# Two heads by turns: pairing the small TensorE products of a hybrid layer's state scan and attentions

## The chip, the cores and the metric

The kernel runs on one core of a Trainium2 chip. The metric is the device time of one execution in microseconds (us); lower is better. Five engines work side by side, each through its own stream of instructions and in its order: TensorE (PE; its weight loads are shown as PEld), VectorE (DVE), ScalarE (ACT), GpSimd (POOL) and SyncE (SP), which here issues most transfers.

## The reference, cut to what matters

Two layers of a diffusion backbone on 384 tokens (128 of context, 256 latent) of width 1024. In each layer one projection of the modulated tokens feeds three token mixers of 8 heads of 64 channels each, which are gated, merged and projected; a retrieval over 16384 experts (PEER) follows.

```python
# A: state scan, one chunk of 128 tokens, per head
y_diag = einsum('bhcls,bcshp->bclhp', cb * Lmat, xd)
y_off = einsum('bclhn,bchpn,bhcl->bclhp', Cc, states, exp(a_cs))
# B: neighbourhood attention, per head
s_loc = einsum('brcqhd,brcijhd->bhrcqij', qb, kb) * scale + bias
s_ctx = einsum('brcqhd,bshd->bhrcqs', qb, ctx_k) * scale
p = softmax(concatenate([s_loc, s_ctx]))
o = einsum(p[..., :n_loc], vb) + einsum(p[..., n_loc:], ctx_v)
# C: grouped attention, 8 query heads on 2 key heads
s = einsum('bqkgd,bskd->bkgqs', qi, k) * scale
o = einsum('bkgqs,bskd->bqkgd', softmax(s), v)
```

## The kernel before

Tokens lie in three tiles of 128 (t = 0 for the context, 1 and 2 latent); channels are folded in chunks of 128, so that a chunk holds two heads, one on partitions 0 to 63 and one on 64 to 127. `hybrid_step` runs `mixer` and `peer` for each of two layers. In `mixer` the projections go through `proj3` (L368 to L370): three products for each of 8 chunks, with the operands split into a high and a low part, each 128 by 128 of weights against 384 columns. `branch` (L675 and on) makes a gate with `proj3` and one mixer's output projection (L685 to L687) for eight chunks. All other products of the mixer are in plain 32-bit floats, and PE runs each of these as two passes: the profile counts two instructions for one call.

The state scan loops over t, then over two groups g, then over two chunks j of a group, then over the two heads h2 of a chunk. For each head DVE makes a weight tile `w1` in three operations (L617 to L619; tag `w1` has 2 buffers), and PE writes three products into the head's half of the PSUM tile `py`: the values against `w1` (L621; 128 rows, 64 columns of the array) and, for t > 0, the carried states of both directions (L626 and L627; 64 rows, 64 columns). DVE then reads both halves (L629).

The neighbourhood attention loops over chunks j, tiles t and heads h2: scores into a tile `ps` (L747, or L751 for the latent and L752 for the cached keys; 64 rows of the array, those of the head, by 128 columns), bias (L755) and copy (L757), `softmax_T` (L403 to L414: maximum, exponential, reciprocal, scaling, transposes on PE at L412, and the copy to `pT` on ACT at L414), and one to three products of the values with `pT` into the head's half of `po` (L761; 128 rows, 64 columns). The output tile `po` is opened ahead of both heads, and is copied out after both (L762).

The grouped attention does the same over c, t and h2, with heads 2c and 2c + 1. Both have the key head kv = c // 2, and so both take the same 64 rows of the array for their scores (L827, L831, L832); the value products are L836, the copy is L837.

`po`, `ps`, `py` and the score tiles of the scan (L589, L600) share the PSUM tag `pa` with 3 buffers; the transposes use `pt` with 2. The order on each engine is not written out: a planner sets it when the program is built. It goes by program order as priority, by what its own estimate of times says is ready, and by free buffers, and so it puts products of `proj3` and `branch`, and the modulation units (`adaln_unit`, L259 and L265), between the small ones. On the chip each engine follows that order and waits where an operand is late.

`blocked` lays the weights out before the launch; `w_branch` holds the output projections of the three mixers.

Of the kernel before, what the change touches and what calls it, by code (L numbers as in the profile page):

```python
# [18 lines left out]
D = 1024  # L19
KD = 8  # L20
NP, NS, NTOK = 128, 256, 384
DEPTH = 2
IN_COLS = 6672
HD = 64
# [131 lines left out]
def hybrid_step(ctx: ExitStack, tc: tile.TileContext, A, O):  # L156
    nc = tc.nc
    V, S, T, G = nc.vector, nc.scalar, nc.tensor, nc.gpsimd
# [259 lines left out]
    def mixer(l, stack, right, ps1):  # L418
# [4 lines left out]
        with ExitStack() as sc0:  # L423
            sp = pool(sc0, "ln")
# [159 lines left out]
        for t in range(3):  # L584
            cb = mk(sp, [128, 2, 128], "cb", bufs=2)
            for g in range(2):
                gs = slice(g * 64, g * 64 + 64)
                psc = mk(ps1, [128, 512], "pa")
                T.matmul(psc[:, :128], xc[gs, 4, t * 128:(t + 1) * 128], xc[gs, 5, t * 128:(t + 1) * 128], start=True, stop=True)  # L589
                S.copy(cb[:, g, :], psc[:, :128])  # L590
            ec = [mk(sp, [128, 4, 128], f"ec{d}") for d in range(2)] if t > 0 else None
            for g in range(2):
                gs = slice(g * 64, g * 64 + 64)
                E = []
                for d in range(2):
                    tri, msk = (triU, maskU) if d == 0 else (triL, maskL)
                    ps = mk(ps1, [128, 512], "pa")
                    for q in range(4):
                        h = d * 8 + g * 4 + q
                        T.matmul(ps[:, q * 128:(q + 1) * 128], a[:, t, h:h + 1].to_broadcast([128, 128]), tri, start=True, stop=True)  # L600
                    p4 = ps.rearrange("p (q l) -> p q l", q=4)
                    if t > 0:
                        S.activation(ec[d][gs], p4[gs], AF.Exp)
                        V.tensor_tensor(ec[d][gs], ec[d][gs], xc[gs, 5, t * 128:(t + 1) * 128][:, None, :].to_broadcast([64, 4, 128]), op=ALU.mult)
                    ex = mk(sp, [128, 4, 128], f"ex{d}")
                    V.tensor_tensor(ex, p4, msk[:, None, :].to_broadcast([128, 4, 128]), op=ALU.add)
                    for q in range(4):
                        h = d * 8 + g * 4 + q
                        S.activation(ex[:, q, :], ex[:, q, :], AF.Exp, bias=csn[:, t, h:h + 1])
                    E.append(ex)  # L610
                for j in (2 * g, 2 * g + 1):
                    py = mk(ps1, [128, 512], "pa")
                    for h2 in range(2):
                        h = 2 * j + h2
                        q = h % 4
                        w1 = mk(sp, [128, 128], "w1", bufs=2)
                        V.tensor_scalar(w1, E[0][:, q, :], dt[:, t, h:h + 1], None, op0=ALU.mult)  # L617
                        V.scalar_tensor_tensor(w1, E[1][:, q, :], dt[:, t, 8 + h:9 + h], w1, op0=ALU.mult, op1=ALU.add)
                        V.tensor_tensor(w1, w1, cb[:, g, :], op=ALU.mult)  # L619
                        o = py[h2 * 64:(h2 + 1) * 64, :128]  # L620
                        T.matmul(o, xnat[:, t, h * 64:(h + 1) * 64], w1, start=True, stop=(t == 0))  # L621
                        if t > 0:
                            jj = q // 2
                            sf = h0T if t == 1 else h1T
                            sb = h1T if t == 1 else h0T
                            T.matmul(o, sf[gs, 0, jj, h2 * 64:(h2 + 1) * 64], ec[0][gs, q, :], start=False, stop=False)  # L626
                            T.matmul(o, sb[gs, 1, jj, h2 * 64:(h2 + 1) * 64], ec[1][gs, q, :], start=False, stop=True)  # L627
                    y = xc[:, j, t * 128:(t + 1) * 128]
                    V.scalar_tensor_tensor(y, y, dvec[:, j:j + 1], py[:, :128], op0=ALU.mult, op1=ALU.add)  # L629
                    V.tensor_tensor(y, y, zT[:, j, t * 128:(t + 1) * 128], op=ALU.mult)  # L630
                    S.activation(sq[:, j, t * 128:(t + 1) * 128], y, AF.Square)
# [96 lines left out]
        for j in range(4):  # L728
            bias2 = []
            for h2 in range(2):  # L730
                h = 2 * j + h2
                bt = mk(sp, [128, 6, 64], "bt", bufs=3)
                for half in range(2):
                    dma(out=bt[half * 64:(half + 1) * 64], in_=AP(rpb, (h * 15 + 5 - half) * 31 - 48, [[1, 64], [31, 6], [1, 64]]))
                pb = mk(ps1, [128, 512], "pt")
                T.matmul(pb[:, :384], flip, bt.rearrange("p r c -> p (r c)"), start=True, stop=True)
                V.tensor_tensor(bt, pb[:, :384].rearrange("p (r c) -> p r c", r=6), colm[:, None, :].to_broadcast([128, 6, 64]), op=ALU.add)
                bias2.append(bt)
            for t in range(3):
                po = mk(ps1, [128, 512], "pa")  # L740
                for h2 in range(2):
                    h = 2 * j + h2
                    hs = slice(h2 * 64, h2 * 64 + 64)
                    ps = mk(ps1, [128, 512], "pa")
                    q = nq[hs, j, t * 128:(t + 1) * 128]
                    if t == 0:
                        T.matmul(ps[:, :128], q, nk[hs, j, 0:NP], start=True, stop=True)  # L747
                        pT = softmax_T(ps[:, :128], 128, sp, ps1)
                        vs = [nv[:, 0, :]]
                    else:  # L750
                        T.matmul(ps[:, 0:256], q, nk[hs, j, NP:NTOK], start=True, stop=True)  # L751
                        T.matmul(ps[:, 256:384], q, ckT[hs, j, :], start=True, stop=True)  # L752
                        sc = mk(sp, [128, 384], "nsc", bufs=2)
                        i0 = 2 - 2 * (t - 1)
                        V.tensor_tensor(sc[:, 0:256].rearrange("p (r c) -> p r c", r=4), ps[:, 0:256].rearrange("p (r c) -> p r c", r=4),  # L755
                                        bias2[h2][:, i0:i0 + 4, :], op=ALU.add)
                        S.copy(sc[:, 256:384], ps[:, 256:384])  # L757
                        pT = softmax_T(sc, 384, sp, ps1)
                        vs = [nv[:, 1, :], nv[:, 2, :], cv]
                    for i, vv in enumerate(vs):  # L760
                        T.matmul(po[hs, :128], vv[:, h * 64:(h + 1) * 64], pT[:, i, :], start=(i == 0), stop=(i == len(vs) - 1))  # L761
                V.tensor_copy(ysT[1][:, j, t * 128:(t + 1) * 128], po[:, :128])  # L762

        branch(0)
# [16 lines left out]
        for t in range(3):  # L781
# [31 lines left out]
            ps = mk(ps1, [128, 512], "pt")  # L813
            T.transpose(ps[:, :128], src[:, 8:10, :].rearrange("p h d -> p (h d)"), ident)
            V.tensor_copy(gkT[:, t * 128:(t + 1) * 128], ps[:, :128])
        for c in range(4):
            for t in range(3):
                po = mk(ps1, [128, 512], "pa")
                for h2 in range(2):
                    h = 2 * c + h2  # L820
                    kv, j = h // 4, h % 4
                    hs = slice(kv * 64, kv * 64 + 64)
                    ps = mk(ps1, [128, 512], "pa")
                    q = gqT[hs, j, t * 128:(t + 1) * 128]
                    if t == 0:
                        n = 128
                        T.matmul(ps[:, :128], q, gkT[hs, 0:NP], start=True, stop=True)  # L827
                        vs = [gn[:, 0, 640:768]]
                    else:
                        n = 384  # L830
                        T.matmul(ps[:, 0:256], q, gkT[hs, NP:NTOK], start=True, stop=True)  # L831
                        T.matmul(ps[:, 256:384], q, gcT[hs, :], start=True, stop=True)  # L832
                        vs = [gn[:, 1, 640:768], gn[:, 2, 640:768], gcv]
                    pT = softmax_T(ps[:, :n], n, sp, ps1)
                    for i, vv in enumerate(vs):
                        T.matmul(po[h2 * 64:(h2 + 1) * 64, :128], vv[:, kv * 64:(kv + 1) * 64], pT[:, i, :], start=(i == 0), stop=(i == len(vs) - 1))  # L836
                V.tensor_copy(ysT[2][:, c, t * 128:(t + 1) * 128], po[:, :128])  # L837
        branch(1)
        branch(2)
# [469 lines left out]
def blocked(inputs):  # L1309
# [14 lines left out]
    d["peer_wq"] = cut(d["peer_wq"], KD, 128)[:, :, 0]  # L1324
    d["w_mod"] = cut(d["w_mod"], 4, 256)
    d["w_out"] = cut(d["w_out"], 4, 256)
    d["w_branch"] = cut(d["w_branch"], 4, 256)[:, :, :, 0]
    return d

# [20 lines left out]
```

## Time and profile before

| | |
|---|---|
| time before, median of 3 runs | 3023.25 us (3023.19 to 3025.1) |
| the profiled execution | 3023.89 us, of which the span from first to last instruction 3021.8 us |
| busy in the span: PE, PEld, DVE, ACT, POOL | 2880.1, 2496.8, 2314.3, 1398.6, 820.5 us |
| mean granted TensorE clock | 0.982 of 2.4 GHz |
| layer 0: state scan, neighbourhood attention, grouped attention | some 112 to 185, 255 to 350, 355 to 442 us |
| layer 1: the same | some 1645 to 1702, 1755 to 1862, 1872 to 1958 us |

A row of the timeline gives the start and the time of merged neighbours, the engine, the line, what is written and read, the size of the weights (partitions by columns), the size of the moving operand, and how many instructions are merged. The time of one matmul goes from its start to its modelled end, and neighbours overlap, so the difference between two starts tells what one costs. In a view by line the columns are: count, busy us, mean ns, then idle time of the engine ahead of the group and who ended it.

### The profile page before, as it was taken

To read this page: it belongs to the slowest core of one execution; us is meant where nothing else is said; L and a number is where in the kernel's file an instruction comes from. 1 tells how busy PE (TensorE), PEld (TensorE's weight loads), DVE (VectorE), ACT (ScalarE), POOL (GpSimd) and SP (SyncE) were. 2 spreads that over 40 slices of the span, in tenths; PEclk is the share of its full clock that TensorE was granted. 3 is DMA by queue.
4 is the path that set the end of the run, shared out by engine and by line. 5 is a ranking of instruction groups with operands and counts; after the bars stand their busy time and mean duration, and the time that the engine had idled before them with its cause. 6 is when DMAs were issued, how large, how long until landed. Compare 5 with 4: busy or idle time off the path is not lost. (4 is left out here: it accounts for less than half of the span.)

```text
span 3021.8 us, 48665 instructions
## 1 busy us (share of the span) xinstructions
PE 2880.1 (95%) x17953; PEld 2496.8 (83%) x17953; DVE 2314.3 (77%) x4888; ACT 1398.6 (46%) x2861; POOL 820.5 (27%) x566
## 2 busy tenths in 40 slices
PE   7999999999889999999969999999987999999996
PEld 5888889878779999998858888898876899999985
DVE  3745554599669999998977456446996999999988
ACT  4544542324864444444445445432168444444443
POOL 0000000101334445554530000000023444455554
PEclk9999999999999999999979999999999999999998
DMA  7445322464999999999934332124469999999994
GB/s 245 156 152 153 84 65 90 154 227 146 334 343 418 393 388 396 396 390 369 385 100 153 119 96 76 64 91 133 154 212 366 412 395 392 396 394 392 395 365 166
DMA packets 299328, 767.09 MB, mean 254 GB/s; under 512 B 42770, under 2 KB 113874, under 8 KB 299090
## 3 DMA queue, kind: packets, MB, share of 16 engines
q1 hardware_dynamic: 225362, 495.51, 46.0%
q0 software_dynamic: 73728, 268.47, 23.4%
q8 instruction: 141, 2.31, 0.3%
q14 instruction: 97, 0.79, 0.1%
HBM read 726.92 MB, written 36.96 MB: 253 GB/s over the span
## 5 line engine op out<-in xcount | busy, mean ns | idle before, releaser
L1052 POOL DMA_INDIRECT prow<-in_peer_u,ei x256 | 361.5, 1412 | 765.2 <-DVE prow L1057 521.6
L1063 POOL DMA_INDIRECT prow<-in_peer_v,ei x256 | 379.8, 1483 | 352.4 <-DVE tn L1068 310.8
L222 ACT CAST vh<-w 128x1024 fp32r<-128x1024 f32 x256 | 268.8, 1050 | 367.2 <-issue 285.6
L1162 PE MATMUL hp<-hh,uh 128*128 128x256 f32 x1488 | 433.8, 292 | 0.0
L1163 PE MATMUL hp<-hl,uh 128*128 128x256 f32 x1488 | 417.2, 280 | 0.0
L1164 PE MATMUL hp<-hh,ul 128*128 128x256 f32 x1488 | 416.8, 280 | 0.0
L1240 PE MATMUL out<-vh,al 128*128 128x512 f32 x1024 | 400.4, 393 | 3.6 <-DVE al L1225 3.6
L1239 PE MATMUL out<-vl,ah 128*128 128x512 f32 x1024 | 398.4, 391 | 3.1 <-DVE vl L224 3.1
L1238 PE MATMUL out<-vh,ah 128*128 128x512 f32 x1024 | 391.0, 398 | 1.4 <-ACT ah L1223 1.4
L224 DVE TENSOR_TENSOR vl<-w,vh 128x1024 fp32r<-128x1024 f32 x256 | 315.5, 1232 | 62.0 <-ACT vh L222 61.3
L1068 DVE SCALAR_TENSOR_TENSOR tn<-prow,pact,tn 128x1024 f32<-128x1024 f32 x254 | 325.0, 1280 | 2.7
L1150 ACT CAST uh<-w 128x1024 fp32r<-128x1024 f32 x186 | 195.4, 1051 | 251.7 <-PE hp L1163 243.0
L368 PE MATMUL pp<-hh,uh 128*128 128x384 f32 (+1 forms) x848 | 300.1, 354 | 8.9 <-ACT uh L222 4.7
L1057 DVE SCALAR_TENSOR_TENSOR prow<-prow,tn 128x1024 f32<-128x1024 f32 x256 | 302.2, 1218 | 0.3 <-DMA prow<-in_peer_u,ei 0.3
L370 PE MATMUL pp<-hh,ul 128*128 128x384 f32 (+1 forms) x848 | 296.3, 349 | 1.4 <-POOL ul L224 1.4
L1159 PE MATMUL hp<-hs,w 128*128 128x256 f32 x1120 | 266.5, 394 | 30.7 <-DMA w<-in_peer_uT 30.7
L369 PE MATMUL pp<-hl,uh 128*128 128x384 f32 (+1 forms) x848 | 295.0, 348 | 0.2 <-DVE xr L494 0.2
L1162 PEld LDWEIGHTS hp<-hh,uh 128*128 128x128 f32 x1488 | 281.3, 189 | 0.0
L1163 PEld LDWEIGHTS hp<-hl,uh 128*128 128x128 f32 x1488 | 281.2, 189 | 0.0
L1164 PEld LDWEIGHTS hp<-hh,ul 128*128 128x128 f32 x1488 | 280.4, 188 | 0.0
L1159 PEld LDWEIGHTS hp<-hs,w 128*128 128x128 f32 x1120 | 216.1, 197 | 63.0 <-DMA w<-in_peer_uT 33.5
L351 POOL TENSOR_TENSOR res<-res,lg 128x384 f32<-128x384 f32 x6 | 9.6, 1594 | 939.7 <-ACT res L313 939.7
(405 smaller groups left out, 5843.0 us busy)
## 6 DMA issues: line engine op xcount, KB each, us to landing
w<-in_peer_uT SPq DMA_DIRECT2D x256, 512.0 KB, 6.9
w<-in_peer_v SPq DMA_DIRECT2D x256, 512.0 KB, 7.2
w<-in_w_in SPq DMA_DIRECT2D x104, 512.0 KB, 3.7
w<-in_w_mod SPq DMA_DIRECT2D x96, 512.0 KB, 4.4
gd<-w SPq DMA_DIRECT2D x64, 512.0 KB, 6.1
gt<-gd SPq DMA_DIRECT2D x64, 512.0 KB, 7.4
w<-in_peer_wq SPq DMA_DIRECT2D x32, 512.0 KB, 4.4
w<-in_w_branch SPq DMA_DIRECT2D x24, 512.0 KB, 3.7
```

The source lines that it names most:

```text
L224: e.tensor_tensor(lo, src, hi.bitcast(F32), op=ALU.subtract)
L1052: G.indirect_dma_start(out=row, out_offset=None, in_=utab, in_offset=bass.IndirectOffsetOnAxis(ap=ei[:, j:j + 1], axis=0))
L1057: V.scalar_tensor_tensor(row, row, 1.0, tn, op0=ALU.mult, op1=ALU.mult, accum_out=hd[:, j:j + 1])
L1063: G.indirect_dma_start(out=row, out_offset=None, in_=vtab, in_offset=bass.IndirectOffsetOnAxis(ap=ei[:, j:j + 1], axis=0))
L1068: V.scalar_tensor_tensor(acc, row, act[:, j:j + 1], acc, op0=ALU.mult, op1=ALU.add)
L1159: T.matmul(o, ut[0][:, k, :], hs[:, k, :], start=(k == 0), stop=(k == KD - 1))
L1162: T.matmul(o, uh[:, k, :], hh[:, k, :], start=(k == 0), stop=False)
L1163: T.matmul(o, uh[:, k, :], hl[:, k, :], start=False, stop=False)
L1164: T.matmul(o, ul[:, k, :], hh[:, k, :], start=False, stop=(k == KD - 1))
L1238: T.matmul(o, ah[:, ts], vh[:, ns], start=f, stop=False)
L1239: T.matmul(o, ah[:, ts], vl[:, ns], start=False, stop=False)
L1240: T.matmul(o, al[:, ts], vh[:, ns], start=False, stop=e)
```

## The change

The state scan makes both heads' weight tiles first (tag `w1` with 4 buffers) and then goes through three steps, each for both heads. Both attentions open two score tiles, compute the scores of both heads by turns, run the softmax of each, and only then open `po` and go through the value products by turns. In the grouped attention the pair is now one head of each key head (c and 4 + c), so that the two lie on other rows; its output chunk c holds those two heads, and `blocked` puts the rows of the third branch's weights into that order.

```diff
                 for j in (2 * g, 2 * g + 1):
                     py = mk(ps1, [128, 512], "pa")
-                    for h2 in range(2):
-                        h = 2 * j + h2
+                    w2 = []
+                    for h in (2 * j, 2 * j + 1):
                         q = h % 4
-                        w1 = mk(sp, [128, 128], "w1", bufs=2)
+                        w1 = mk(sp, [128, 128], "w1", bufs=4)
...
-                        o = py[h2 * 64:(h2 + 1) * 64, :128]
-                        T.matmul(o, xnat[:, t, h * 64:(h + 1) * 64], w1, start=True, stop=(t == 0))
-                        if t > 0:
-                            jj = q // 2
-                            sf = h0T if t == 1 else h1T
-                            sb = h1T if t == 1 else h0T
-                            T.matmul(o, sf[gs, 0, jj, h2 * 64:(h2 + 1) * 64], ec[0][gs, q, :], start=False, stop=False)
-                            T.matmul(o, sb[gs, 1, jj, h2 * 64:(h2 + 1) * 64], ec[1][gs, q, :], start=False, stop=True)
+                        w2.append(w1)
+                    sf, sb = (h0T, h1T) if t == 1 else (h1T, h0T)
+                    jj = (j % 2)
+                    for step in range(1 if t == 0 else 3):
+                        for h2, w1 in enumerate(w2):
+                            h = 2 * j + h2
+                            o, hc = py[h2 * 64:(h2 + 1) * 64, :128], slice(h2 * 64, (h2 + 1) * 64)
+                            if step == 0:
+                                T.matmul(o, xnat[:, t, h * 64:(h + 1) * 64], w1, start=True, stop=(t == 0))
+                            elif step == 1:
+                                T.matmul(o, sf[gs, 0, jj, hc], ec[0][gs, h % 4, :], start=False, stop=False)
+                            else:
+                                T.matmul(o, sb[gs, 1, jj, hc], ec[1][gs, h % 4, :], start=False, stop=True)
...
+            hv = [slice(h2 * 64, h2 * 64 + 64) for h2 in range(2)]
             for t in range(3):
-                po = mk(ps1, [128, 512], "pa")
-                for h2 in range(2):
...
+                pss = [mk(ps1, [128, 512], "pa") for _ in range(2)]
+                q = nq[:, j, t * 128:(t + 1) * 128]
+                keys = [(0, nk[:, j, 0:NP])] if t == 0 else [(0, nk[:, j, NP:NTOK]), (256, ckT[:, j, :])]
+                for o, kk in keys:
+                    for hs, ps in zip(hv, pss):
+                        T.matmul(ps[:, o:o + kk.shape[-1]], q[hs], kk[hs], start=True, stop=True)
+                pTs = []
+                for h2, ps in enumerate(pss):
...
+                po = mk(ps1, [128, 512], "pa")
+                for i, vv in enumerate(vs):
+                    for h2, hs in enumerate(hv):
+                        h = 2 * j + h2
+                        T.matmul(po[hs, :128], vv[:, h * 64:(h + 1) * 64], pTs[h2][:, i, :], start=(i == 0), stop=(i == len(vs) - 1))
...
+        hv = [slice(kv * 64, kv * 64 + 64) for kv in range(2)]
         for c in range(4):
             for t in range(3):
+                pss = [mk(ps1, [128, 512], "pa") for _ in range(2)]
+                q = gqT[:, c, t * 128:(t + 1) * 128]
...
+                for o, kk in keys:
+                    for hs, ps in zip(hv, pss):
+                        T.matmul(ps[:, o:o + kk.shape[-1]], q[hs], kk[hs], start=True, stop=True)
+                pTs = [softmax_T(ps[:, :n], n, sp, ps1) for ps in pss]
                 po = mk(ps1, [128, 512], "pa")
...
+                for i, vv in enumerate(vs):
+                    for hs, pT in zip(hv, pTs):
+                        T.matmul(po[hs, :128], vv[:, hs], pT[:, i, :], start=(i == 0), stop=(i == len(vs) - 1))
...
+    wb = d["w_branch"].copy()
+    wb[:, 2] = wb[:, 2].reshape(DEPTH, 2, 4, HD, D).transpose(0, 2, 1, 3, 4).reshape(DEPTH, 512, D)
+    d["w_branch"] = wb
     d["w_branch"] = cut(d["w_branch"], 4, 256)[:, :, :, 0]
```

## Rows read from the trace of the kernel before

**Rows 1.** Part 1 of the page: busy us, share of the span, instructions.

```profile
PE 2880.1 (95%) x17953; PEld 2496.8 (83%) x17953; DVE 2314.3 (77%) x4888; ACT 1398.6 (46%) x2861; POOL 820.5 (27%) x566
```

**Rows 2.** Windows of layer 0's state scan, neighbourhood and grouped attention.

```profile
core 0: us, PE busy (x) PEld busy (x) DVE busy (x) ACT busy (x) POOL busy (x), PEclk, DMA share, GB/s
112.00:185.00 73.00, 72.90 (x492) 58.35 (x490) 47.82 (x124) 37.79 (x102) 0.00 (x0) 1.00 0.35 118
255.00:350.00 95.00, 94.42 (x575) 76.41 (x574) 57.38 (x137) 42.63 (x108) 0.00 (x0) 1.00 0.41 108
355.00:442.00 87.00, 86.26 (x500) 71.15 (x500) 51.12 (x119) 40.84 (x96) 0.00 (x0) 1.00 0.19 61
```

**Rows 3.** Timeline of PE in the state scan, one pair of heads.

```profile
139.52 0.33 PE L369 MATMUL pp<-hl,uh 128*128 128x384 f32 x1
139.69 0.34 PE L370 MATMUL pp<-hh,ul 128*128 128x384 f32 x1
139.96 0.43 PE L621 MATMUL pa<-w,xnat 128*64 128x128 f32 x2
140.32 0.43 PE L626 MATMUL pa<-ec,h0T 64*64 64x128 f32 x2
...
140.90 0.43 PE L621 MATMUL pa<-w,xnat 128*64 128x128 f32 x2
...
141.84 0.44 PE L368 MATMUL pp<-hh,uh 128*128 128x384 f32 x1
142.12 0.34 PE L369 MATMUL pp<-hl,uh 128*128 128x384 f32 x1
```

**Rows 4.** Timeline of PE in the grouped attention.

```profile
391.50 0.43 PE L836 MATMUL pa<-pT,gn 128*64 128x128 f32 x2
391.86 0.45 PE L369 MATMUL pp<-hl,uh 128*128 128x384 f32 x1
...
392.41 0.65 PE L836 MATMUL pa<-pT,gn 128*64 128x128 f32 x4
392.90 0.38 PE L836 MATMUL pa<-pT,gcv 128*64 128x128 f32 x2
393.21 0.70 PE L831 MATMUL pa<-gkT,gqT 64*128 64x256 f32 x2
...
394.71 0.44 PE L368 MATMUL pp<-hh,uh 128*128 128x384 f32 x1
```

**Rows 5.** Timeline of PE in the neighbourhood attention: two visits with scores.

```profile
266.79 0.71 PE L751 MATMUL pa<-nk,nq 64*128 64x256 f32 x4
...
267.65 0.44 PE L369 MATMUL pp<-hl,uh 128*128 128x384 f32 x1
...
276.99 0.48 PE L751 MATMUL pa<-nk,nq 64*128 64x256 f32 x1
...
277.83 0.44 PE L369 MATMUL pp<-hl,uh 128*128 128x384 f32 x1
```

**Rows 6.** Timeline of PE at L589: two products together, and one alone.

```profile
131.23 0.49 PE L589 MATMUL pa<-xc 64*128 64x128 f32 x4
131.65 0.62 PE L259 MATMUL pp<-w,condT 128*32 128x256 f32 x2
...
157.39 0.49 PE L589 MATMUL pa<-xc 64*128 64x128 f32 x2
157.80 0.43 PE L621 MATMUL pa<-w,xnat 128*64 128x128 f32 x2
```

**Rows 7.** Timeline of PE at a modulation unit.

```profile
63.03 1.07 PE L259 MATMUL pp<-w,condT 128*32 128x256 f32 x16
64.03 0.44 PE L368 MATMUL pp<-hh,uh 128*128 128x384 f32 x1
```

**Rows 8.** Timeline of ACT: the probabilities of two heads in flight together.

```profile
272.16 0.48 ACT L414 COPY pT<-pt 128x384 f32<-128x384 f32 x1
...
275.60 0.48 ACT L414 COPY pT<-pt 128x384 f32<-128x384 f32 x1 [2.69 <-PE pt L412]
```

**Rows 9.** Groups by line: idle time ahead of L761's loads and of L617.

```profile
L761 PEld LDWEIGHTS pa<-pT,nv 128*64 128x64 f32 x160 | 16.2, 135 | 13.1 <-ACT pT L414 10.9 <-issue 1.8 <-ACT uh L222 0.3
...
L617 DVE TENSOR_SCALAR w<-ex,dt 128x128 f32<-128x128 f32 x48 | 12.5, 280 | 7.2 <-PE pa L621 7.2
```

More of the change, by code (lines that the diff above doesn't have):

```diff
@@ L738, in mixer @@
                 bias2.append(bt)
+            hv = [slice(h2 * 64, h2 * 64 + 64) for h2 in range(2)]
             for t in range(3):
-                po = mk(ps1, [128, 512], "pa")
-                for h2 in range(2):
[L742 to L745, printed above, removed]
+                pss = [mk(ps1, [128, 512], "pa") for _ in range(2)]
[6 more added lines that the diff above has]
+                for h2, ps in enumerate(pss):
                     if t == 0:
-                        T.matmul(ps[:, :128], q, nk[hs, j, 0:NP], start=True, stop=True)
-                        pT = softmax_T(ps[:, :128], 128, sp, ps1)
-                        vs = [nv[:, 0, :]]
-                    else:
-                        T.matmul(ps[:, 0:256], q, nk[hs, j, NP:NTOK], start=True, stop=True)
-                        T.matmul(ps[:, 256:384], q, ckT[hs, j, :], start=True, stop=True)
+                        pTs.append(softmax_T(ps[:, :128], 128, sp, ps1))
+                    else:
                         sc = mk(sp, [128, 384], "nsc", bufs=2)
@@ L757, in mixer @@
                         S.copy(sc[:, 256:384], ps[:, 256:384])
[L758 to L761, printed above, removed]
+                        pTs.append(softmax_T(sc, 384, sp, ps1))
+                vs = [nv[:, 0, :]] if t == 0 else [nv[:, 1, :], nv[:, 2, :], cv]
+                po = mk(ps1, [128, 512], "pa")
[3 more added lines that the diff above has]
+                        T.matmul(po[hs, :128], vv[:, h * 64:(h + 1) * 64], pTs[h2][:, i, :], start=(i == 0), stop=(i == len(vs) - 1))
                 V.tensor_copy(ysT[1][:, j, t * 128:(t + 1) * 128], po[:, :128])
@@ L815, in mixer @@
             V.tensor_copy(gkT[:, t * 128:(t + 1) * 128], ps[:, :128])
+        hv = [slice(kv * 64, kv * 64 + 64) for kv in range(2)]
         for c in range(4):
             for t in range(3):
-                po = mk(ps1, [128, 512], "pa")
[L819 to L836, printed above, removed]
+                pss = [mk(ps1, [128, 512], "pa") for _ in range(2)]
+                q = gqT[:, c, t * 128:(t + 1) * 128]
+                if t == 0:
+                    n, keys, vs = 128, [(0, gkT[:, 0:NP])], [gn[:, 0, 640:768]]
+                else:
+                    n, keys, vs = 384, [(0, gkT[:, NP:NTOK]), (256, gcT)], [gn[:, 1, 640:768], gn[:, 2, 640:768], gcv]
+                for o, kk in keys:
+                    for hs, ps in zip(hv, pss):
+                        T.matmul(ps[:, o:o + kk.shape[-1]], q[hs], kk[hs], start=True, stop=True)
+                pTs = [softmax_T(ps[:, :n], n, sp, ps1) for ps in pss]
+                po = mk(ps1, [128, 512], "pa")
+                for i, vv in enumerate(vs):
+                    for hs, pT in zip(hv, pTs):
+                        T.matmul(po[hs, :128], vv[:, hs], pT[:, i, :], start=(i == 0), stop=(i == len(vs) - 1))
                 V.tensor_copy(ysT[2][:, c, t * 128:(t + 1) * 128], po[:, :128])
```

## The prediction

> **What bounds the kernel now.** I read the page's busy times first. TensorE (PE) is busy for 95% of the span [rows 1], so the question is whether it is also what the changed stages wait for. The windows say yes: in the state products (SSD), the neighbourhood attention (NA) and the grouped attention (GQA) of layer 0, PE has work for 72.9 of 73, 94.4 of 95 and 86.3 of 87 us, at a granted clock of 1.00, which is the 2.4 GHz level, while VectorE (DVE) has 48, 57 and 51 us [rows 2]. The planner fills every gap between small products with the big 384-column products of the projections. So in these stages a microsecond taken out of PE's own stream comes off the time, as long as there is filling, and the filling is only moved, not used up. Layer 1 repeats the pattern.
>
> Busy time can't price the small products, since they overlap; I went to the timeline and took differences between starts. A filling product follows the last by 0.17 us (139.52 to 139.69). Then the state products of one pair of heads: 139.96 to 141.84, 1.88 us. One head takes 0.36 for its value product (L621, 128 rows by 64 columns of the array) and 0.58 for its two state products (L626 and L627, 64 by 64). Each change of shape costs: L621 starts 0.27 after the filling product before it and not 0.17, and the second filling product after the run starts 0.28 after the first. A visit of small products among the filling so costs about 0.20 on top of its own time [rows 3].
>
> The attention rows show the contrast on which the forecast stands. In GQA two heads that share a key head lie on the same 64 rows, and their scores run one after the other: L831 and L832 of one head, then of the next, 393.21 to 394.71, 1.50 us. In NA the scores of two neighbouring heads lie on opposite rows, and both, in the same shapes, are through in 0.86 us, 266.79 to 267.65 [rows 4, 5]. The same stands at L589: two products on opposite rows take 0.42 us and one alone takes 0.41 [rows 6]. For columns, 16 passes of 128 by 32 (L259), spread over four column groups, take 1.00 us, 0.06 each, where one pass alone has 256 columns to stream [rows 7]. A partner on other rows or columns is nearly free.
>
> **Part by part.**
>
> *GQA scores.* There are 4 head pairs, 2 late token tiles (t of 1 and 2) and 2 layers: 16 places. The new pairs have one head from each key head, so opposite rows: 1.50 becomes 0.86 as NA shows, 0.64 each, 10.2 us. The first tile's 128-column scores I leave at nothing.
>
> *NA scores.* These overlap today already, by luck of the order: head 1 of one tile runs with head 0 of the next. Three such visits per pair of heads cost 0.86, 0.84 (276.99 to 277.83) and about the same, 2.55; the new pairs cost 0.42 and twice 0.86, 2.14 [rows 5, 6]. That is 0.4 for 8 pairs, 3.3 us.
>
> *Value products of both attentions.* Today each head has its own run of three, 0.80 us (392.41 to 393.21), or one alone, 0.36 (391.50 to 391.86) [rows 4]. Afterwards the two heads come by turns into the two column halves of one PSUM tile. But the probabilities of the two heads aren't ready together: their copies (L414) start at 272.16 and 275.60, 3.44 us apart [rows 8]. The planner issues what is ready, so I expect the first head's first product alone (0.36), filling, and then the other five side by side in the time of three (0.80): 1.16 against 1.60 today. That saves 0.44 for 16 places in each attention, 14.1 us. The lower end is nothing (the heads stay apart), the upper is 0.80 and one visit less, 1.00 each, with 0.56 for each of 16 first tiles, 41 us. I take 14, since the 3.44 us row is the nearest one.
>
> *State products.* There are 16 pairs with carried state (4 pairs, 2 tiles, 2 layers). The two value products now stand side by side, then the forward and the backward state products of both heads. If both weight tiles are ready, a pair costs 0.36 + 0.58 = 0.94, and 0.94 is saved; if the first value product goes alone, 0.36 + 0.94 and a second visit, and 0.38 is saved. Today the two heads' runs stand without filling between them, and DVE waits 7.2 us for L621 to give a weight buffer back [rows 3, 9], which the change from 2 to 4 buffers takes away; both speak for the first, and DVE's turn per head for the second. I take the middle, 0.66, so 10.5 us (6 to 15). No row has two 64 by 64 products on the same rows and different columns. If they don't overlap, 0.44 of each 0.58 comes back, 7 us; the nearest row, L259, says they do. The first tile's value products I leave at nothing.
>
> *What costs nothing.* The third branch's weight rows are put in order before the launch; the chip loads the same bytes. The output tile is opened later, at its first product. Scores of the next tile need the two freed score tiles out of three, and today they already come right behind a value run [rows 4, 5]; the filling covers a late one, 0.17 a piece. If that cover went, each wait would count in full.
>
> *Sum.* 10.2 + 3.3 + 14.1 + 10.5 = 38 us. The profiled execution took 3023.9 us (span 3021.8), 0.6 over the median. 3023.9 - 38 is 2986.
>
> **Rivals.**
>
> *The planner keeps the heads apart* (the change doesn't do what it says). If products into different halves of a tile may pass each other, the planner takes the first head's remaining products when they are ready and the turns never happen. For it: the 3.44 us. Against it: it must then treat two writes into one PSUM tile as independent, which no row shows. Only the scores gain, 13.5 us, with little more: 3009.
>
> *All pairs meet.* If PE lags behind the planner's clock, both heads are ready when it comes. For it: state runs without filling between them [rows 3]. Against: 3.44 us. Then value products save 41, states 15, scores 13.5: 70 us, 2954.
>
> *Passes in strict order.* A product here is two passes. If the passes of one product stand together in PE's stream and PE starts them in that order only, a pair can share one pass and not both, and each block of pairs takes one pass more, 0.12 us (four passes of L836 take 0.49, 392.41 to 392.90). For some 128 blocks (48 of scores, 48 of values, 32 of states) that is 15 us: 3001. Against it: the second product of L589 costs 0.01 and not 0.12 [rows 4, 6]. The rows don't show the order of the passes in the stream. The Trainium skill, "TensorE: Matmul & The Clock Gate", Part 3, states this rule: matmuls start and end strictly in program order, and overlap only where a later one sits on another tile of the array. The rows of L589 speak against it as far as they go.
>
> *PE stands at the second head* (slower). PE issues in order. If the planner thinks the second head's probabilities earlier than the chip has them, PE waits in front of the second product of the turn, with the next scores and all filling queued behind it. The price is the wait itself: 48 places (24 per layer). It decides from 38 / 48 = 0.8 us each; at a third of the 3.44 us, 1.15 us, it costs 55 and gives 3041. Against it: before L761's 160 weight loads with the new values only 10.9 us are waits for these copies today [rows 9], since the planner puts filling there.
>
> **How the numbers follow.** Forecast (2986, with 2970 to 3000 its own range) 0.48; heads kept apart 0.20; all meet 0.12; strict order 0.05; no change beyond 0.2%, about what a measurement can tell (6 us: the gain is given back by a reshuffled order elsewhere) 0.08; PE stands 0.07. The first four are faster, 0.85. The range reaches from the case where all meet to the one where the heads stay apart, 2950 to 3012, and leaves out some 0.18.
>
> **What would show it.** Right: L831 and L832 of two heads in about 0.86 us; value products in one run of ten passes of about 0.80 behind one of two; state runs of a pair at 0.94 to 1.30; PE still 99% busy in the three stages, each shorter: over both layers SSD by about 10, NA by 10, GQA by 17 us. Wrong: value runs of six passes as today (planner); runs of twelve (all meet); idle time of PE in front of L761's or L836's successors that names the copy L414 (PE stands); a GQA score pair still at 1.5 us would say that opposite rows don't overlap there and would take the base from the forecast.

## The result, and the profile after

The changed kernel takes 3002.74 us (median of 4 executions, 2999.95 to 3004.09) against 3023.22 beside it, a ratio of 0.9933 (95% interval 0.9915 to 0.995). The forecast was 2986 in a range of 2950 to 3012: the direction is right, and about half of the 38 us came. The profiled execution took 3004.09 us (span 3002.3), 19.8 less than that of before.

Part 1 of the page, and windows of the three stages of layer 0, with two stretches inside the scan (columns as in [rows 2]). The last row is from the profile of before, the ten microseconds behind the scan window of [rows 2]:

```profile
PE 2855.6 (95%) x17953; PEld 2479.3 (83%) x17953; DVE 2309.1 (77%) x4888; ACT 1396.8 (47%) x2861; POOL 824.8 (27%) x566
```

```profile
112.00:181.00 69.00, 66.86 (x445) 54.83 (x444) 44.42 (x125) 36.09 (x98) 0.00 (x0) 0.89 0.29 95
137.60:147.80 10.20, 10.16 (x47) 8.04 (x48) 3.98 (x13) 2.18 (x8) 0.00 (x0) 0.52 0.26 99
175.60:182.40 6.80, 6.80 (x29) 6.47 (x26) 2.04 (x4) 3.17 (x5) 0.00 (x0) 0.50 0.22 72
255.00:345.00 90.00, 88.47 (x563) 70.02 (x562) 55.20 (x133) 42.70 (x110) 0.00 (x0) 1.00 0.36 101
355.00:435.00 80.00, 79.92 (x507) 66.18 (x506) 48.57 (x115) 38.63 (x91) 0.00 (x0) 1.00 0.21 67
```

```profile
185.00:195.00 10.00, 10.00 (x60) 8.34 (x60) 1.97 (x5) 3.28 (x5) 0.00 (x0) 0.83 0.17 54
```

Against [rows 1, 2]: PE lost 24.5 us of busy time with the same 17953 instructions. The grouped attention is still full (79.92 of 80 us); in the neighbourhood attention 1.5 us are idle. In the scan PE idles for some 2 us, and two stretches of 10.2 and 6.8 us run at a granted clock of 0.50 to 0.52, the 1.2 GHz level. The first has no counterpart before, where the scan's window showed 1.00. The second has a shorter one: behind the scan of before the clock is 0.83 over 10 us, which makes some 3.4 us at half.

The timeline of PE in the grouped attention, at the place that answers to [rows 4] (L836 are now the scores, L841 the value products):

```profile
369.73 0.43 PE L841 MATMUL pa<-pT,gn 128*64 128x128 f32 x2
370.10 0.70 PE L836 MATMUL pa<-gkT,gqT 64*128 64x256 f32 x2
370.72 0.54 PE L841 MATMUL pa<-pT,gn 128*64 128x128 f32 x5
...
371.11 0.48 PE L841 MATMUL pa<-pT,gcv 128*64 128x128 f32 x3
371.52 0.48 PE L836 MATMUL pa<-gkT,gqT 64*128 64x256 f32 x1
371.53 0.48 PE L836 MATMUL pa<-gcT,gqT 64*128 64x128 f32 x2
...
372.37 0.44 PE L368 MATMUL pp<-hh,uh 128*128 128x384 f32 x1
```

The value products came as forecast: the first head's first product alone (369.73, two passes), then ten passes of both heads (370.72 to 371.52, 0.80 us). But between the two stands one score product of the *next* tile (370.10), the first keys of one head, alone for 0.62 us. Its partner comes only behind the block, beside the first head's second keys (371.52 to 372.37). The pair of scores is torn. Over both attentions and layers, 22 of the 32 pairs with 384 keys are torn like this, and 4 of the 16 with 128 keys. From 369.73 to 372.37 the place takes 2.64 us. The forecast's own pieces for it are 0.36 + 0.80 + 0.86 = 2.02.

The timeline of PE in the scan: one pair at full clock, as [rows 3] showed it at 1.88 us, and, earlier, the first pair with carried state:

```profile
137.64 0.54 PE L628 MATMUL pa<-w,xnat 128*64 128x128 f32 x4 [2.06 <-DVE w L619]
138.11 0.69 PE L630 MATMUL pa<-ec,h0T 64*64 64x128 f32 x4
...
139.64 0.52 PE L369 MATMUL pp<-hl,uh 128*128 128x384 f32 x1
139.96 0.52 PE L370 MATMUL pp<-hh,ul 128*128 128x384 f32 x1
...
170.56 0.44 PE L628 MATMUL pa<-w,xnat 128*64 128x128 f32 x4
170.93 0.43 PE L630 MATMUL pa<-ec,h1T 64*64 64x128 f32 x4
171.20 0.39 PE L632 MATMUL pa<-ec,h0T 64*64 64x128 f32 x4
171.51 0.44 PE L369 MATMUL pp<-hl,uh 128*128 128x384 f32 x1
```

Timeline of DVE ahead of the wait, and a row of PE's waits (engine, line, what for; us in total, times, longest):

```profile
135.16 1.21 DVE L224 TENSOR_TENSOR ul<-w,uh 128x1024 fp32r<-128x1024 f32 x1
...
137.21 0.48 DVE L619 TENSOR_TENSOR w<-w,cb 128x128 f32<-128x128 f32 x2
```

```profile
PE pt L741 <- DMA bt<-in_na_rpb: 2.9, 4, 0.9
```

At 170.56 the whole pair takes 0.95 us, half of before. At 137.64 PE had stood still for 2.06 us for a weight tile (L619), ahead of the pair's first product: DVE first does a weight split (L224) and then makes both heads' tiles step by step (L619 x2), so that the first is hardly earlier than the second. Right behind the wait the clock falls: filling products follow each other in 0.32 us (139.64 to 139.96), not 0.17. The last row is in the neighbourhood attention, where PE waits for the transfer of a bias table; before there was no such wait.

To see where the time went, I took the differences between the starts of neighbouring matmuls, put each to the line of the earlier one, and summed over both layers (differences over 3 us count as 3; a wait goes to the row of the product ahead of it). The last two columns are experiments below, named by what they change.

| us between starts | before | after | late head first | late head first, in the scan too |
|---|---|---|---|---|
| value products | 62.4 | 50.4 | 37.0 | 37.3 |
| scores | 51.0 | 49.3 | 34.1 | 34.2 |
| state scan, the three lines | 35.1 | 26.7 | 26.3 | 20.6 |
| filling (`proj3`, `branch`) | 609.7 | 599.9 | 601.9 | 605.1 |
| L600, bias (L741), transposes (L412) | 51.4 | 60.2 | 57.9 | 56.3 |
| modulation units | 104.2 | 104.4 | 105.6 | 103.1 |

Value products gave 12.0 (forecast 14.1), the scan 8.4 (10.5), the scores 1.7 (13.5): 3.6 less in the grouped attention and 1.8 more in the neighbourhood attention. The row of the value products holds the 2.9 us of waits for the bias tables, so the products alone gave some 15. The filling gave 9.8 that no term had, as it is broken by small products at 227 places and no longer at 288.

### The profile page after: what moved, and what is told of

Read it like the earlier page. It is cut to its first block, busy times and chain, and to the rows that moved or that the text cites. A ratio compares the mean times of both kernels' runs of the same rounds, so it can differ in the third digit from the quotient of the medians.

```text
span 3002.3 us, 48719 instructions
## 1 busy us (share of the span) xinstructions
PE 2855.6 (95%) x17953; PEld 2479.3 (83%) x17953; DVE 2309.1 (77%) x4888; ACT 1396.8 (47%) x2861; POOL 824.8 (27%) x566
## 4 chain that ended last, share of the span: by engine, by line
PE 74%; DVE 11%; DMA 6%; ACT 4%; issue 4%; POOL 1%; SPq 0%; POOLq 0%; ACTq 0%; DVEq 0%
PE hp L1167 6%; PE out L1243 6%; PE hp L1169 6%; PE out L1245 6%; PE hp L1168 6%; PE out L1244 6%; PE pp L368 5%; PE pp L369 5%; PE pp L370 5%; PE hp L1164 4%; DMA w<-in_peer_uT 3%; PE pp L947 2%; ACT ol L1004 2%; DVE vl L224 2%; DVE tn L1073 2%
## 5 line engine op out<-in xcount | busy, mean ns | idle before, releaser
L224 DVE TENSOR_TENSOR vl<-w,vh 128x1024 fp32r<-128x1024 f32 x256 | 315.8, 1234 | 62.7 <-ACT vh L222 44.0
L224 DVE TENSOR_TENSOR ul<-w,uh 128x1024 fp32r<-128x1024 f32 x124 | 149.8, 1208 | 162.2 <-ACT uh L222 158.2
```

The source lines that it names most:

```text
L224: e.tensor_tensor(lo, src, hi.bitcast(F32), op=ALU.subtract)
```

## The experiments

The theory: the order that the planner wrote keeps the products themselves as cheap as forecast and loses the scores, since an early first value product leaves a hole that a next score product falls into. Rivals: the products don't pair as the rows of before say; a lack of PSUM tiles tears the scores; the scan takes the gain back.

**Halves of the change.** First the attentions as changed with the scan of before, then the reverse.

```diff
# attentions only: the state products go back to one head after the other
-                    for step in range(1 if t == 0 else 3):
-                        for h2, w1 in enumerate(w2):
+                    for h2 in range(2):
...
# scan only: both attentions and the weight rows as before
-                for o, kk in keys:
-                    for hs, ps in zip(hv, pss):
+                for h2 in range(2):
...
```

Attentions only, expected:

> Both attentions as in the changed kernel, the state scan as before. Theory A (the gain is TensorE time taken out of the attentions; the scan's 8 us of product time are eaten by its stall of 2 us per layer and by the half-rate clock behind it): 3000 to 3005 us, as fast as the whole change. Rival B (the gain is the scan's, and the attentions' value gain is given back by the split scores): 3010 to 3018 us.

Scan only, expected:

> The state scan as in the changed kernel, both attentions as before. Theory A: 3018 to 3026 us, no gain, with the stall of about 2 us before L628 and longer stretches at half clock in the trace. Rival B: 3008 to 3015 us.

Measured: 3003.83 us (0.9933, interval 0.992 to 0.9947) and 3019.22 us (0.9986, 0.9976 to 0.9997), beside 3023.72. The attentions alone bring what the whole change does. The scan alone brings 4.5 us, though its products start 9.1 us closer (26.0 against 35.1), and on top of the attentions it shows nothing (3002.74 against 3003.83). Its trace has the same wait at L628, 4.1 us in two places, with half clock behind it. That these take back the rest fits; no run here separates them.

**The late head first.** The turns of the value products begin with the second head, whose probabilities come last. So nothing can start before both are there.

```diff
-                    for h2, hs in enumerate(hv):
+                    for h2, hs in reversed(list(enumerate(hv))):
...
-                    for hs, pT in zip(hv, pTs):
+                    for hs, pT in reversed(list(zip(hv, pTs))):
```

> The changed kernel with one edit: in the value turns of both attentions head 1 comes ahead of head 0, so that no value product is ready before both heads' probabilities are, and the next tile's scores follow a whole block. Theory (the split of the turn is what held the gain down): a place with t > 0 costs 2.64 us now (369.73 to 372.37) and then 0.80 + 0.86; 0.98 less at 32 places, so 31 us under the changed kernel, 2967 to 2975 us. Rival (the longer way from one tile's scores to the next's bounds the stage): TensorE idle before the value products, time within 5 us of the changed kernel, 2998 to 3008 us. Rival (turns as such pay, adjacency doesn't): no forecast from it here.

Measured: 2973.0 us (0.9834, 0.9818 to 0.9851). The timeline of PE at a place of the grouped attention in this kernel:

```profile
377.59 0.66 PE L841 MATMUL pa<-pT,gn 128*64 128x128 f32 x8
378.08 0.39 PE L841 MATMUL pa<-pT,gcv 128*64 128x128 f32 x4
378.40 0.70 PE L836 MATMUL pa<-gkT,gqT 64*128 64x256 f32 x4
378.93 0.39 PE L836 MATMUL pa<-gcT,gqT 64*128 64x128 f32 x4
379.25 0.44 PE L691 MATMUL pb<-ya,uh 128*128 128x384 f32 x1
```

All twelve value passes take 0.81 us, all eight score passes 0.85, together 1.66 against 2.64. The same products in one other order are worth 29.7 us (3002.74 to 2973.0). The table puts 13.4 of it to the values and 15.2 to the scores. No pair of scores is torn in this trace, and the 26 torn ones account for the 15.2: 22 times the 0.62 us of a lone first product (370.10 to 370.72) and 4 times 0.41 with 128 keys (377.50 to 377.91, below). So it was not the products that failed to pair.

**The late head first in the scan too.** As above, and in addition:

```diff
-                        for h2, w1 in enumerate(w2):
+                        for h2, w1 in reversed(list(enumerate(w2))):
```

> As the run above, and in the scan's first step too head 1 comes ahead of head 0, so that no pair of value products is split (half of the 16 pairs with state are now). Theory: 0.4 to 0.6 us for 8 pairs, 3 to 5 us under the run above, and more if the stall of 2 us per layer and the half-clock stretch behind it go: 2957 to 2970 us. Rival (VectorE makes the weights too late, so a pair that waits for both only stalls more): equal to the run above or up to 8 us over it.

Measured: 2969.96 us (0.9824, 0.981 to 0.9838), the fastest version of this study, though its executions (2967.46 to 2974.61) overlap those of the one above. Its scan gives 14.5 us between starts against before (20.6). Its waits of PE (engine, line, what for; us in total, times, longest) and the row of the timeline at the same place:

```profile
PE pp L368 <- ACT nq L655: 4.6, 2, 2.3
...
PE pa L628 <- DVE w L619: 0.6, 2, 0.3
```

```profile
135.87 0.45 PE L368 MATMUL pp<-hh,uh 128*128 128x384 f32 x1 [2.28 <-ACT nq L655]
```

The wait for the weight tile went from 4.1 us (2 times) to 0.6, and another took its place ahead of a filling product, 2.28 us once in each layer. Stretches at half clock remain (6.8 us from 137.6 on). The medians differ by 3.0 us, of the some 6 that the products gained; with the overlap of the executions the 3.0 are not clear of the scatter.

**Is it the number of PSUM tiles?** The changed kernel with 4 buffers for the scores and outputs (tag `pa`) and 1 for the transposes:

```diff
-{"pp": 2, "pt": 2, "pa": 3, "pb": 1}
+{"pp": 2, "pt": 1, "pa": 4, "pb": 1}
```

> The changed kernel with 4 buffers of the PSUM tag pa and 1 of pt (3 and 2 before). Asked of the trace alone: if the next tile's scores are torn apart because a score tile is missing, both heads' scores now stand whole behind the first value product, about 0.86 us; if they are torn apart because the rest of the value turn outranks them, a lone score product still stands between the first value product and the other five. The time I expect within 10 us of the changed kernel either way, since one transposing buffer less delays the softmaxes.

Measured: 3002.78 us, one execution. The timeline of PE in its grouped attention, ahead of a tile with 384 keys and ahead of one with 128:

```profile
364.91 0.70 PE L836 MATMUL pa<-gkT,gqT 64*128 64x256 f32 x2
365.54 0.54 PE L841 MATMUL pa<-pT,gn 128*64 128x128 f32 x5
...
366.34 0.48 PE L836 MATMUL pa<-gkT,gqT 64*128 64x256 f32 x1
...
372.39 0.43 PE L841 MATMUL pa<-pT,gn 128*64 128x128 f32 x2
372.75 0.49 PE L836 MATMUL pa<-gkT,gqT 64*128 64x128 f32 x4
373.18 0.54 PE L841 MATMUL pa<-pT,gn 128*64 128x128 f32 x5
```

In the changed kernel the place with 128 keys looked like this:

```profile
377.50 0.48 PE L836 MATMUL pa<-gkT,gqT 64*128 64x128 f32 x2
377.91 0.54 PE L841 MATMUL pa<-pT,gn 128*64 128x128 f32 x5
...
378.71 0.48 PE L836 MATMUL pa<-gkT,gqT 64*128 64x128 f32 x2
```

So the rival holds for the short scores: with a buffer more, both heads' 128-key scores stand whole in the hole (372.75), at 16 of 16 places instead of 12. It doesn't hold for the long ones: one head's first product still stands alone (364.91), at 26 of 32 places, and was so at 22. The scores of this trace add up to 52.4 us, not fewer than the 49.3 of the changed kernel. A buffer more doesn't mend the tearing as a whole; what does is that the block can't begin early.

**Is it the turns, or only the block?** Late head first, but three products of one head and then three of the other:

```diff
-                for i, vv in enumerate(vs):
-                    for h2, hs in reversed(list(enumerate(hv))):
+                for h2, hs in reversed(list(enumerate(hv))):
+                    for i, vv in enumerate(vs):
```

> As late_first, but the value products are written head by head: all three of head 1, then all three of head 0, next to each other. Theory (adjacency in one shape of the array is what pays; TensorE starts products on other columns side by side even when they stand three calls apart): a value block still takes about 0.80 us, 2969 to 2978 us. Rival (passes start strictly in the order of the stream): the block takes about 1.3 to 1.4 us, 0.55 more at 32 places, 17 us over late_first, 2987 to 2994 us.

Measured: 2979.75 us (0.9856, 0.9837 to 0.9875), between both theories. The timeline of PE:

```profile
378.02 0.71 PE L841 MATMUL pa<-pT,gn 128*64 128x128 f32 x6
378.50 0.27 PE L841 MATMUL pa<-pT,gcv 128*64 128x128 f32 x1
378.56 0.27 PE L841 MATMUL pa<-pT,gn 128*64 128x128 f32 x1
378.61 0.27 PE L841 MATMUL pa<-pT,gcv 128*64 128x128 f32 x1
378.67 0.27 PE L841 MATMUL pa<-pT,gn 128*64 128x128 f32 x1
378.78 0.38 PE L841 MATMUL pa<-pT,gcv 128*64 128x128 f32 x2
379.09 0.70 PE L836 MATMUL pa<-gkT,gqT 64*128 64x256 f32 x4
```

The block takes 1.07 us, where turns take 0.81 and two heads apart 1.60 (0.80 each, [rows 4]). For 32 blocks the 0.26 more is 8.3 us; 6.8 were measured. So most of the overlap doesn't need the turns: products of one head (`gn` at 378.56 and 378.67) start among the last products of the other (`gcv` at 378.50 and 378.61), though the program writes all of the latter's first. PE's planned stream itself is not on record. That the planner kept this order is inferred from the changed kernel, where it left the first head's other two products waiting for their turn.

**What are other rows worth?** The late-head version, with the pairs of the grouped attention as before: two neighbouring heads, both on the 64 rows of one key head; the third branch's weights in the old order.

```diff
-                q = gqT[:, c, t * 128:(t + 1) * 128]
+                ks = hv[c // 2]
...
-                    for hs, ps in zip(hv, pss):
-                        T.matmul(ps[:, o:o + kk.shape[-1]], q[hs], kk[hs], start=True, stop=True)
+                    for h2, ps in enumerate(pss):
+                        T.matmul(ps[:, o:o + kk.shape[-1]], gqT[ks, (2 * c + h2) % 4, t * 128:(t + 1) * 128], kk[ks], start=True, stop=True)
```

> The value turns begin with the late head (whole blocks, as in late_first, 2973.0 us), but in the grouped-query attention a pair is again two neighbouring heads, whose score products use the same 64 rows; the weight rows of the third branch keep their old order. Theory: other rows are worth what the two score visits differ by, 1.50 us on the same rows against 0.85 on other rows, 0.65 in each of 16 places of 384 keys and some 0.2 in each of 8 places of 128 keys: 10.4 + 1.6 = 12 us. So 2981 to 2988 us. Rival, after the run that had only the other rows and whose median stayed at the time of before: the time in the score visits comes back elsewhere, and this kernel takes 2970 to 2977 us.

Measured: 2983.24 us (0.9876, 0.986 to 0.9892), 10.2 more than with other rows (by the recorded ratios 12.7). The timeline of PE:

```profile
380.38 0.66 PE L841 MATMUL pa<-pT,gn 128*64 128x128 f32 x8
380.87 0.39 PE L841 MATMUL pa<-pT,gcv 128*64 128x128 f32 x4
381.18 1.13 PE L836 MATMUL pa<-gkT,gqT 64*128 64x256 f32 x4
382.15 0.60 PE L836 MATMUL pa<-gcT,gqT 64*128 64x128 f32 x4
382.69 0.44 PE L691 MATMUL pb<-ya,uh 128*128 128x384 f32 x1
```

The value block is the same 0.80 us; the scores take 1.51 where other rows take 0.85. Two heads by turns on the same rows don't overlap at all (1.50 in [rows 4], one after the other). Summed over the grouped attention the scores start 12.1 us closer with other rows (29.1 to 17.0), those of the first tiles included. Here the forecast's price for the grouped scores stands.

**The other rows alone, in the kernel before.** Only the pairing of heads and the weight rows change; the order of the loops stays.

```diff
-                    kv, j = h // 4, h % 4
+                    kv, j = h2, c
```

> The kernel before with one edit: in the grouped attention the pair of heads is c and 4 + c (with the weight rows in that order), so that neighbours lie on opposite rows; the old order of products stays. Theory: two scores in a row fall from 1.50 to 0.86 us at 16 places, 10 us less, and a little more at places with a first tile: 3009 to 3015 us. Rival (the row change needs the turns): 3020 to 3026 us.

The same kernel once more, expected:

> The kernel before with the other pairs of heads in the grouped-query attention, a second look. Its first profiled execution took 3012.6 us, with 6 us less between the starts of its score products than before; the median of its 12 executions was 3023.4. Theory: the 6 us are there in each execution and other stretches vary by more from one to the next: the median of the executions is 3014 to 3022, and this profile again shows score products at 18 us in all. Rival: the gain is given back behind them in most executions: 3021 to 3026, and a profile of such an execution shows score products at 18 us and the waits of another line longer by as much.

Measured: 3023.37 us (0.9996, 0.9986 to 1.0006, 12 executions from 3012.59 to 3027.44), then 3020.92 (0.9991, 0.998 to 1.0001, 11 executions). Both intervals hold 1, so no gain is shown. The first expectation was wrong; the second median lies at the top of the theory's range, just below the rival's. In the two profiles the grouped scores start 7.1 us closer (29.7 to 22.6) and not 10, since the order of before sets two 384-key scores of the grouped attention side by side at 8 places and not at 16. Yet the time from the first to the last filling product of each mixer, added over both layers, shrinks by 1.7 and 1.1 us only. The waits of PE have, in both profiles, a row that was nearly nothing before (0.7 us, 4 times):

```profile
PE pt L412 <- DVE p L409: 3.8, 12, 0.5
```

With the scores done sooner PE arrives at the transposes ahead of the probabilities. That is 3.1 us of the 7.1. In the measure of the table it lies in the filling, which takes 4.4 and 5.1 us more than before at the same 288 places, and the row with the transposes takes 0.9 more. Why the filling grows by the rest stays open; the medians are 1.1 and 2.8 us below those of before.

**Can earlier fills close the scan's wait?** `N_FIRST` is the number of weight splits at the start of a mixer that go to GpSimd (POOL) and not to DVE, which makes the late weight tile. The best version with 16 for 3:

```diff
-N_FIRST = 3
+N_FIRST = 16
```

> As both_late_first, with the weight splits of the first 16 projections of a layer (3 before) subtracted on the idle GpSimd and not on VectorE. Theory (the scan's stalls come from VectorE's queue, where a 1.22 us split stands ahead of the weight tiles): the stalls of about 2 us per layer and part of the half-clock stretches go, 2960 to 2967 us. Rival (ScalarE's queue, exponentials and copies, holds the filling up): within 3 us of both_late_first; slower than 2973 if GpSimd's splits come late.

Measured: 3017.73 us (0.9973, 0.9964 to 0.9982), 48 us more than with 3: the expectation was wrong. Its waits of PE, its group of splits on POOL (line, engine, operation, shapes; busy us and mean ns; idle before), and its scan window:

```profile
PE pp L368 <- ACT xr L499: 15.6, 5, 4.5
...
PE pa L628 <- DVE w L619: 12.8, 8, 3.6
```

```profile
L224 POOL TENSOR_TENSOR ul<-w,uh 128x1024 fp32r<-128x1024 f32 (+1 forms) x32 | 73.5, 2303 | 199.4 <-ACT uh L222 178.2 <-PE pp L259 13.4 <-PE pp L370 7.9
```

```profile
50.00:180.00 130.00, 111.30 (x674) 94.42 (x675) 84.05 (x162) 53.51 (x133) 35.33 (x16) 0.86 0.36 123
```

A split on POOL takes 2.3 us. PE is busy for 111.30 of these 130 us at 0.86, where the best version has 126.57 at 0.93. The wait for the weight tile didn't fall but grew, from 0.6 to 12.8 us. The edit moved many more pieces of work than the one that was late, so it doesn't settle whether the wait comes from DVE's queue.

## Why the prediction was right in sign and half in size

**What bounds the kernel.** Right. PE stays nearly full in the attentions, and what leaves its stream leaves the time: the table's rows sum to 22.9, 51.0 and 57.2 us less than before in its three other columns, and the times are 20.5, 50.7 and 53.8 less.

**Grouped and neighbourhood scores, 10.2 + 3.3.** This is the step that failed, by 11.8 of the missing 17 us. Not the price: two heads on opposite rows take 0.85, on the same rows 1.51, and in the late-head version that difference is 10.2 us of time. That this is the very figure of the sum is luck: it holds the first tiles too, which the sum left out (between the starts the difference is 12.1 us, of which 16 times 0.66 are 10.6). What failed is the sentence that the next tile's scores "already come right behind a value run", so that they cost nothing to place. I had split the value run into a lone product and five others, and didn't ask what the planner puts into the hole. It puts a score product of one head there, and its partner runs 1.4 us later (370.10 and 371.52). In place of 10.2 + 3.3 the grouped scores gave 3.6 and the neighbourhood scores lost 1.8.

**Value products, 14.1.** Right in pattern, the runs of two and ten passes, at all 32 places, and near in size: some 15, of which the waits for the bias tables, a term that the sum didn't have, take 2.9 back.

**State products, 10.5.** Right in its parts: a full pair takes 0.95 us (0.94 forecast), others come split, as at the lower bound, and the starts are 8.4 us closer. But I costed the change of buffers as only a gain. PE now waits for a weight tile, 4.1 us in two places, and runs the work behind it at half clock. The rival "PE stands at the second head" is near to this, but PE stands ahead of the pair's first product, since DVE makes both tiles together. In the attentions no wait for the second head's probabilities shows, but the one for the bias tables does.

**What costs nothing.** Wrong in the other direction as well: fewer breaks in the filling gave 9.8 us. That is about what L600 (3.5 more), bias (3.4) and transposes (1.9) took back.

**The other rivals.** *Heads kept apart* fell: the value runs hold both heads in one block. *All pairs meet* (2954) is not what this change does. The late head first makes the pairs meet at every place, and even so it stops at 2973: the values give 25.4 us where that rival had 41, the scores 16.9 where it had 13.5. *Strict order of passes* fell: full pairs cost no extra pass (0.81 for twelve, 0.80 for six before), and in the by-head version products seem to start ahead of earlier ones. The range held because it reached up to the case in which only some of the terms come.

## What to carry to other kernels

A pair of small products saves only while both stand together in the stream, so ask of each pair which partner is ready first and what the scheduler will put into the gap. Opening a block with the operand that comes last keeps it whole; here this one word of order was worth more (29.7 us) than the whole rewrite (20.5). A price taken from a clean row of the trace can be trusted further than the place where one assumes that the instruction will stand.

## What the runs showed of the hardware

**Starts out of the stream's order.** The by-head rows above have `gn` passes of the head that the program writes last starting ahead of the other head's last `gcv`, on the other 64 columns. The Trainium skill, "TensorE: Matmul & The Clock Gate", Part 3, says that matmuls start and end strictly in program order. If the stream stands as the program writes it, which is inferred above and not on record, these rows disagree: products on other columns start ahead of their turn, but not all the way, since the block takes 1.07 us and not 0.81.

**Pairs of 64 by 64.** No row of before had two such products on the same rows and other columns. Step two and three of a pair take 0.58 us for four products (170.93 to 171.51), as two did before [rows 3]: they overlap fully.

**The clock.** It stood at 2.4 GHz through layer 0's scan before, to 185 us [rows 2], and here it fell to 1.2 GHz for 10.2 us right behind an idle time of PE of 2.06 us; after a wait of 2.28 us in the best version it also fell, for 6.8 us. So a short wait in this stage can cost more than itself: at 0.32 us for 0.17, ten microseconds of filling are worth some 5. The second stretch has no idle time ahead of it: PE had been busy with a run of products of a single column, here as before, where the clock fell behind it too (the 0.83 above).

```profile
172.24 2.39 PE L641 MATMUL pa<-ones,xr 128*128 128x1 f32 x20
```

**Changing the shape.** A break in the filling costs about 0.2 us beside the products in it, before and after (369.47 to 369.73, then 372.37 to 372.65, against 0.17 each). The Trainium skill, "TensorEngine Tiling (Array Packing)", Key Properties, says that a change of tiling mode drains TensorE. The rows fit that; they show the added 0.2 us and not what PE does in it.
